# The queries' rank as a seven-product unit, and the values of heads 2 and 3 computed early and parked in memory

## The chip, the cores and the metric

The kernel runs on one core of a Trainium2 chip. Its engines work in parallel, each through its own list in order, and wait for each other by semaphores: TensorE (PE) does matrix products into PSUM, VectorE (DVE) and ScalarE (ACT) do everything elementwise, GpSimd (POOL) does a little, and SyncE (SP) issues the transfers between memory and the on-chip buffer, also in order. The metric is device time in microseconds (us) of one execution.

## The reference

One layer of a hybrid encoder over 512 tokens of width 2048. The input is normalised to `h`, and one wide projection makes all that follows:

```python
proj = h @ w_in[layer]
(a_q, a_f, a_i, a_g, c_q, c_kv, k_idx_raw, w_idx_raw, b_g, m_a, m_b) = jnp.split(proj, SPLIT_POINTS, axis=-1)
y_a = hgrn2_branch(a_q, a_f, a_i, a_g, ...)          # 8 heads of 128
y_b = dsa_branch(c_q, c_kv, k_idx_raw, w_idx_raw, b_g, ...)
merged = sigmoid(m_a) * (y_a @ w_pa) + sigmoid(m_b) * (y_b @ w_pb)
out = rmsnorm(x + merged @ w_out)
```

Branch A is a gated linear recurrence: per head a state is decayed by `f` and fed with `k` and the values `v` (`a_i`), in chunks. Branch B is sparse attention. The queries' rank `c_q` (512 wide) is normalised by its root mean square and projected to the attention's queries and the indexer's; the latent `c_kv` (256 wide) is normalised and projected to keys and values; the indexer's key `k_idx_raw` (128 wide) goes through a layer norm. The indexer scores all keys for each query, and the best 128 are kept.

## The kernel before

Everything is held transposed: features on the partitions, tokens along the free dimension. Products in float32 are done as three products of halves: each operand is split into a high part (`hi`, a rounded copy made by ACT) and a low part (`lo`, the difference, made by DVE); `mm3` (L93) adds high by high, high by low and low by high. `split` (L89) is that pair of instructions.

**Jobs and pumps.** The program is a list of jobs that are run one after the other. A job is a projection: it loads weights in blocks through SP (`load`, two raw buffers), splits them two blocks ahead of their use (`prep`, three buffers for each half), and issues the products block by block. After each part of a block it calls `pump` (L221), which issues pending loads and stores and moves each of the *lanes* one step on. A lane is a queue of generators with the work that runs beside the projections: norms, the recurrence of two heads (`hgrn_gen`, L767), the selection of the best keys (`top_gen`), attention (`att_gen`). So the order on each engine is written by hand, in steps of a pump. The recurrence has 17 steps. `top_gen` gets 2.7 credits a pump less `R.load`, which the recurrence sets to what its step costs on DVE, and spends 0.94, 1.21 or 1.48 on each of 48 selection steps.

**Kinds of job.** `feat_job` makes tiles of 128 features by 512 tokens, 48 products of 512 columns each; `ai_job` makes the values of two heads with tokens on the partitions, 192 products of 256 columns. `pair_job` (`pair_unit`, L1192) makes four feature tiles at once with seven products where eight would be needed: features and tokens are cut in two and sums of the quarters are multiplied, in all 336 products of 256 columns. It needs sums of the weights (`pair_sums`, L158) and sums of x (`pair_gen`, L1144: eight pieces, `s0` to `s7`, in three steps each). Its results are combined by seven DVE instructions, and stored (`pair_evac`, L1217).

**The order around the change.** A start stage written out by hand normalises x and makes the values of heads 0 and 1. Then come `feat_job`s for half of the rank, the indexer's key, the other half of the rank, and the latent, with the sums of x, the norm of the key and the sum of squares of the rank beside them; the seven-product units of the gates and of heads 4 to 7 (13 units; the normalised rank is reloaded and split beside the third and fourth); the indexer; `end_index`; values of heads 6 and 7, values of 4 and 5, `f` and `q` of heads 0 and 1, values of 2 and 3, `f` and `q` of heads 2 and 3; `open_att` (L1300), which drains all recurrences but one and puts the attention's buffers where theirs lay; the attention's queries (`uq_evac`) and keys and values (`ukv_job`) of two heads; one job of gates (`gate_job`, L1246) with a hook that drains the last recurrence; the output projections.

Four PSUM banks (`mmp`) turn over among the tiles of all jobs; four more (`sdp`) serve the lanes.

Of the kernel before, what the change touches and what calls it, by code (L numbers as in the profile page):

```python
# [63 lines left out]
EVEN = 0  # L64
MO = (0, 128, 384, 768)
# [3 lines left out]
def hybrid_block(ctx, tc, x, norm_w, w_in, lb_table, gnorm_a, q_norm_w, kv_norm_w, w_uq,  # L69
# [51 lines left out]
    cq_d = dram.tile([4, 128, T], F32, name="cq_d")  # L121
    qf_d = dram.tile([2, 4, 128, T], F32, name="qf_d")
# [400 lines left out]
    def cq_evac(j0):  # L523
        def evac(c, ps):
            t = R.cq[:, j0 + c, :]
            A.activation(t, ps, AF.Copy)
            late[1].append(lambda: SP.dma_start(cq_d[j0 + c], t))
        return evac

    def kx_evac(c, ps):  # L530
        A.activation(R.kx[:, 0, :], ps, AF.Copy)

    def ckv_evac(c, ps):
        t = R.g.tile([128, 2, 256], F32, name=f"c{c}").rearrange("p a b -> p (a b)")
        A.activation(t, ps, AF.Copy)
        late[1].append(lambda: SP.dma_start(ckv_d[c], t))
# [7 lines left out]
    def q_sums(j0):  # L544

        for j in (j0, j0 + 1):
            s = R.i.tile([128, T], F32, name="nsq", bufs=2)
            A.activation(s, R.cq[:, j, :], AF.Square)
            if j == 0:
                R.qs = R.i.tile([128, T], F32, name="qs")  # L550
                first = s
            elif j == 1:
                V.tensor_add(R.qs, first, s)
            else:
                V.tensor_add(R.qs, R.qs, s)
        if j0 == 0:
            yield
            return
        sh = R.i.tile([128, T], FR, name="sumh")
        sl = R.i.tile([128, T], FR, name="suml")  # L560
        split(sh, sl, R.qs)
        yield
        yield
        ps = bank("ns")
        mm(ps, ones_r, sh, True, False)
        mm(ps, ones_r, sl, False, True)
        rstd_row(ps, 512, R.rq)
        yield
# [43 lines left out]
    def kidx_gen():  # L612
        def spread(src):
            sh = R.i.tile([128, T], FR, name="sumh")
            sl = R.i.tile([128, T], FR, name="suml")
            split(sh, sl, src)
            yield
            ps = bank("ns")
            mm(ps, ones_r, sh, True, False)
            mm(ps, ones_r, sl, False, True)  # L620
            return ps

        ps = yield from spread(R.kx[:, 0, :])
        t = R.i.tile([128, T], F32, name="nt", bufs=2)
# [1041 lines left out]
```

## Time and profile before

| | us |
|---|---|
| median of 3 runs | 1343.94 (1342.82 to 1344.22) |
| profiled execution | 1345.55 |
| its span, first to last instruction | 1343.8 |
| PE busy | 1331.4 (99%) |
| DVE busy | 1088.4 (81%) |
| ACT busy | 691.4 (51%) |
| transfers | 202.10 MB, mean 150 GB/s |

The profile is of one execution. A row of its timeline gives the start and the duration of one instruction in microseconds, the engine, the line of the kernel, the operation and what it writes and reads (`out<-in`, buffer numbers left out); in square brackets stands how long the engine had been idle before, and what it waited for. Neighbouring matmuls overlap in such rows, so that start to start is the price of one. A row of windows gives the stretch, its length, then for PE, PEld (weight loads), DVE, ACT and POOL the busy time with the number of instructions, the granted clock of PE as a share of full speed, the share of the transfer engines and GB/s.

### The profile page before, as it was taken

The page shows a single profiled execution, that of the slowest core. Times are in us where ns is not written, and L with a number is a line of the kernel's source. Part 1 is how long each engine was busy: PE and PEld are TensorE (multiplying, and loading weights), DVE is VectorE, ACT ScalarE, POOL GpSimd, SP SyncE. Part 2 cuts the span into 40 slices and gives each one's busy share as a digit, 9 for nine tenths or more (in the row PEclk, how much of TensorE's full clock was granted, in tenths as well). Part 3 has the DMA queues.
Part 4 walks back from the last instruction along what each step waited for, and adds up shares of the span by engine and source line. Part 5 has one row for each costly group of instructions (what it writes and reads, how often), then busy time and mean ns, then how long its engine had stood idle before and what let it go on. Part 6 is the DMA issues. An engine that isn't in the chain of part 4 may idle for free.

```text
span 1343.8 us, 27088 instructions
## 1 busy us (share of the span) xinstructions
PE 1331.4 (99%) x11058; PEld 1243.0 (93%) x11058; DVE 1088.4 (81%) x1764; ACT 691.4 (51%) x1115; POOL 51.7 (4%) x63
## 2 busy tenths in 40 slices
PE   8999999999999999999999999999999999999997
PEld 8888999999999999999999898888888888899996
DVE  7978889988898888886778887975656658899997
ACT  7555445545554445445756554655433434354455
POOL 0000000000000000000000000020101100001112
PEclk9999999999999999999999999999999999999999
DMA  7245345544453454446214433445856556654643
GB/s 226 71 118 145 108 142 173 158 141 142 127 154 105 138 154 142 143 143 207 85 51 140 132 106 96 126 136 172 289 167 202 181 187 212 212 174 148 194 145 126
DMA packets 143326, 202.10 MB, mean 150 GB/s; under 512 B 10545, under 2 KB 83810, under 8 KB 143074
## 3 DMA queue, kind: packets, MB, share of 16 engines
q1 hardware_dynamic: 142914, 200.12, 47.5%
q8 instruction: 86, 1.41, 0.4%
q14 instruction: 38, 0.31, 0.1%
q10 hardware_dynamic: 288, 0.26, 0.1%
HBM read 166.25 MB, written 35.66 MB: 150 GB/s over the span
## 4 chain that ended last, share of the span: by engine, by line
PE 97%; DVE 1%; DMA 0%; ACT 0%; issue 0%; SPq 0%; DVEq 0%; ACTq 0%
PE pp L94 16%; PE pp L95 16%; PE pp L96 16%; PE acc L94 14%; PE acc L96 13%; PE acc L95 13%; PE acc L99 2%; PE hl L99 1%; PE ho L99 1%; PE sc L94 1%; PE sc L95 1%; PE sc L96 1%; DMA x<-in_x_dram 0%; PE pt L374 0%; PE hp L99 0%; PE po L96 0%
## 5 line engine op out<-in xcount | busy, mean ns | idle before, releaser
L171 ACT ACTIVATE wh<-sv 128x512 fp32r<-128x512 f32 x264 | 158.6, 625 | 114.4 <-DVE sv L164 85.4
L169 ACT ACTIVATE bh<-wr 128x768 fp32r<-128x768 f32 x132 | 111.5, 845 | 197.6 <-issue 91.8
L95 PE MATMUL pp<-s,wh 128*128 128x256 f32 x624 | 172.6, 277 | 0.0
L94 PE MATMUL pp<-s,wh 128*128 128x256 f32 x624 | 172.6, 277 | 0.0
L96 PE MATMUL pp<-s,wl 128*128 128x256 f32 x624 | 172.6, 277 | 0.0
L173 DVE TENSOR_TENSOR wl<-sv,wh 128x1024 fp32r<-128x1024 f32 x132 | 161.2, 1221 | 5.4
L172 DVE TENSOR_TENSOR bl<-wr,bh 128x768 fp32r<-128x768 f32 x132 | 126.0, 954 | 37.7 <-ACT bh L169 37.3
L94 PE MATMUL acc<-xh,wh 128*128 128x512 f32 x304 | 121.0, 398 | 0.0
L96 PE MATMUL acc<-xh,wl 128*128 128x512 f32 x304 | 118.8, 391 | 0.0
L95 PE MATMUL acc<-xl,wh 128*128 128x512 f32 x304 | 118.6, 390 | 0.0
L95 PEld LDWEIGHTS pp<-s,wh 128*128 128x128 f32 x624 | 117.2, 188 | 0.0
L96 PEld LDWEIGHTS pp<-s,wl 128*128 128x128 f32 x624 | 117.2, 188 | 0.0
L94 PEld LDWEIGHTS pp<-s,wh 128*128 128x128 f32 x624 | 117.2, 188 | 0.0
L95 PE MATMUL pp<-xl,bh 128*128 128x256 f32 x416 | 115.1, 277 | 0.0
L96 PE MATMUL pp<-xh,bl 128*128 128x256 f32 x416 | 115.0, 277 | 0.0
L94 PE MATMUL pp<-xh,bh 128*128 128x256 f32 x416 | 115.0, 277 | 0.0
L91 DVE TENSOR_TENSOR wl<-wr,wh 128x1024 fp32r<-128x1024 f32 (+1 forms) x70 | 84.0, 1201 | 28.8 <-ACT wh L90 28.7
L90 ACT ACTIVATE wh<-wr 128x1024 fp32r<-128x1024 f32 (+1 forms) x70 | 72.3, 1033 | 61.6 <-PE acc L95 38.1
L164 DVE TENSOR_TENSOR sv<-wr 128x512 f32<-128x512 f32 x132 | 92.7, 702 | 10.3 <-DMA wr<-in_w_in_dram 6.9
L94 PE MATMUL acc<-yh,wh 128*128 128x512 f32 x256 | 100.3, 392 | 0.0
L96 PE MATMUL acc<-yh,wl 128*128 128x512 f32 x256 | 99.9, 390 | 0.0
L95 PE MATMUL acc<-yl,wh 128*128 128x512 f32 x256 | 99.9, 390 | 0.0
(391 smaller groups left out, 3769.9 us busy)
## 6 DMA issues: line engine op xcount, KB each, us to landing
wr<-in_w_in_dram SPq DMA_DIRECT2D x136, 512.0 KB, 3.7
wr<-in_w_out_dram SPq DMA_DIRECT2D x28, 512.0 KB, 3.9
mg<-gate_d SPq DMA_DIRECT2D x48, 256.0 KB, 5.3
gate_d<-c SPq DMA_DIRECT2D x44, 256.0 KB, 5.2
wr<-in_w_in_dram SPq DMA_DIRECT2D x36, 256.0 KB, 3.1
wr<-in_w_pa_dram SPq DMA_DIRECT2D x16, 512.0 KB, 5.4
wr<-in_w_pb_dram SPq DMA_DIRECT2D x16, 512.0 KB, 4.0
wr<-in_w_qidx_dram SPq DMA_DIRECT2D x8, 512.0 KB, 4.5
```

Source lines behind the costliest of these rows:

```text
L90: A.activation(hi, src, AF.Copy)
L91: V.tensor_tensor(lo, src, hi.bitcast(F32), op=OP.subtract)
L94: PE.matmul(ps, lh, rh, start=first, stop=False, skip_group_check=True)
L95: PE.matmul(ps, lh, rl, start=False, stop=False, skip_group_check=True)
L96: PE.matmul(ps, ll, rh, start=False, stop=last, skip_group_check=True)
L99: PE.matmul(ps, l, r, start=first, stop=last, skip_group_check=True)
L164: V.tensor_tensor(sv[:, 0:2, :], b[:, 1:3, :], b[:, 0:1, :].to_broadcast([128, 2, 256]), op=OP.add)
L169: A.activation(bh, b[:, 1:4, :], AF.Copy)
L171: A.activation(vh[:, i:i + 2, :], sv[:, i:i + 2, :], AF.Copy)
L172: V.tensor_tensor(bl, b[:, 1:4, :], bh.bitcast(F32), op=OP.subtract)
L173: V.tensor_tensor(vl, sv, vh.bitcast(F32), op=OP.subtract)
```

## The change

- The rank's four feature tiles are no longer two `feat_job`s but one `pair_job`, the first seven-product unit. Its raw result goes to memory (`cq_d`) as before.
- The jobs behind the start are now the latent, the indexer's key, the values of heads 2 and 3 (`ai_job(1, early=True)`, with its weights split as in the other jobs), then the unit of the rank.
- The early values are stored in memory (`v_d`) and loaded when the recurrence of heads 2 and 3 begins. Their job behind the indexer is gone.
- The sums of x are made in two steps a piece, seven pieces before the first unit (`pair_early`) and the eighth inside it (`pair_late`).
- The indexer's key is stored (`kx_d`); its norm, the sum of squares of the rank (`q_squares`, from reloaded pieces) and the scaling of the rank (`q_rows`, unchanged) run one after the other beside the units of the gates, in buffers that are free there.
- The selection starts one job earlier, ahead of the values of heads 6 and 7, with 2.9 credits a pump, less one while the latent's norm runs.
- The attention's first queries are computed ahead of `open_att` and held in PSUM; `open_att` evacuates them, and fixes the order of the attention's buffers.

```diff
+    def q_squares():
+        for j0 in (0, 2):
+            for _ in range(3):
+                yield
+            ts = [R.g.tile([128, 2, 256], F32, name=f"c{i}").rearrange("p a b -> p (a b)") for i in range(2)]
+            for i, t in enumerate(ts):
+                SP.dma_start(t, cq_d[j0 + i])
+            yield
+            yield
+            for t in ts:
+                A.activation(t, t, AF.Square)
...
+        sh, sl = R.cqh[:, 3, :], R.cql[:, 3, :]
+        split(sh, sl, R.rq)
+        yield
+        ps = row_sums(sh, sl)
...
-                    credit += 2.7 - R.load
+                    credit += 2.9 - R.load - bool(lanes["norm"])
...
+            if early:
+                for i in range(2):
+                    t = R.g.tile([128, 2, 256], F32, name=f"c{i}")
+                    A.activation(t, ps[i].rearrange("p (t n) -> p t n", t=2), AF.Copy)
+                    SP.dma_start(v_d[:, 2 * i:2 * i + 2, :], t)
+                return
...
+        if p == 1:
+            hg[p, "v"] = R.v.tile([128, 4, 256], F32, name="hv", bufs=2)
+            SP.dma_start(hg[p, "v"], v_d)
...
+    def pair_early():
+        for k in range(EARLY):
+            a = R.i.tile([128, 2, T], F32, name="xa", bufs=2)
+            V.tensor_tensor(a, *pair_rows(k), op=OP.add)
             d = R.i.tile([128, 4, 256], F32, name="sv", bufs=2)
+            pair_sums_of([a[:, i, j:j + 256] for i in (0, 1) for j in (0, 256)], [d[:, i, :] for i in range(4)])
+            yield
+            hi, hi4, lo, lo4 = sums_place(k)
             df = d.rearrange("p q n -> p (q n)")
+            split(hi, lo, df[:, 0:768] if hi4 is not None else df)
...
+            yield
+
+    def pair_late():
+        for k in range(EARLY, 8):
+            ae, ao, da, db = (R.g.tile([128, 2, 256], F32, name=f"c{i}") for i in range(4))
...
     lane("misc", lb_gen)
-    lane("misc", pair_gen)
-    feat_job(w_in, 4096, 2, NK, 4, x_rhs, cq_evac(0))
-    lane("norm", lambda: q_sums(0))
+    lane("misc", pair_early)
+    feat_job(w_in, 4608, 2, NK, 4, x_rhs, ckv_evac)
     feat_job(w_in, 4864, 1, NK, 4, x_rhs, kx_evac)
-    lane("norm", kidx_gen)
-    feat_job(w_in, 4352, 2, NK, 4, x_rhs, cq_evac(2))
-    lane("norm", lambda: q_sums(2))
-    feat_job(w_in, 4608, 2, NK, 4, x_rhs, ckv_evac)
+    ai_job(1, early=True)
+    lane("misc", pair_late)
+    pair_job(w_in, [4096, 4352], NK // 2, x_pair, pair_evac([cq_d[0:2], cq_d[2:4]], [None, None]))
+    for gen in (kidx_gen, q_squares, q_rows):
+        lane("norm", gen)
...
         leave("norms")
         R.a = enter("att")
+        for n in ("aq0", "av0", "av1", "ak0", "aq1", "ak1"):
+            R.a.tile([128, 2, T] if n[1] != "v" else [128, 4, 256], FR, name=n)
+        for c, ps in enumerate(held):
+            uq_evac(0)(c, ps)
...
     jobs.append(end_index)
+    lane("top", top_gen)
     ai_job(3)
-    lane("top", top_gen)
     ai_job(2)
     af_aq(0)
-    ai_job(1)
     af_aq(1)
+    held = []
+    uq_job(0, lambda c, ps: held.append(ps))
     jobs.append(open_att)
-    uqkv(0)
+    ukv_job(0)
```

More of the change, by code (lines that the diff above doesn't have):

```diff
@@ L520, in lb_gen @@
         yield
[L523 to L528, printed above, removed]
     def kx_evac(c, ps):
[L531 removed]
+        t = R.i.tile([128, T], F32, name="kx")
+        A.activation(t, ps, AF.Copy)
+        late[1].append(lambda: SP.dma_start(kx_d, t))
     def ckv_evac(c, ps):
[L534 removed]
+        t = R.i.tile([128, T], F32, name=f"ck{c}")
         A.activation(t, ps, AF.Copy)
@@ L542, in rstd_row, with row_sums @@
         return r
[L544 to L553, printed above, removed]
-            else:
-                V.tensor_add(R.qs, R.qs, s)
-        if j0 == 0:
-            yield
[L558 to L563, printed above, removed]
+    def q_squares():
[9 more added lines that the diff above has]
+                A.activation(t, t, AF.Square)
+            if j0 == 0:
+                V.tensor_add(R.rq, *ts)
+            else:
+                V.tensor_add(ts[0], *ts)
+                V.tensor_add(R.rq, R.rq, ts[0])
+            for _ in range(3):
+                yield
[3 more added lines that the diff above has]
+        ps = row_sums(sh, sl)
+        for _ in range(2):
+            yield
+        rstd_row(ps, 512, R.rq)
+        for _ in range(5):
+            yield
+    def row_sums(sh, sl):
         ps = bank("ns")
@@ L612, in kidx_gen @@
     def kidx_gen():
[L613 to L616, printed above, removed]
+        t, parts = R.rq, (R.cqh[:, 2, :], R.cql[:, 2, :])
+        SP.dma_start(t, kx_d)
+        for _ in range(3):
             yield
[L618 to L624, printed above, removed]
-        V.scalar_tensor_tensor(t, ps, -1.0 / 128, R.kx[:, 0, :], op0=OP.mult, op1=OP.add)
-        s = R.i.tile([128, T], F32, name="nsq", bufs=2)
+        split(*parts, t)
+        yield
+        ps = row_sums(*parts)
+        for _ in range(2):
+            yield
+        V.scalar_tensor_tensor(t, ps, -1.0 / 128, t, op0=OP.mult, op1=OP.add)
+        for _ in range(4):
+            yield
+        s = R.g.tile([128, 2, 256], F32, name="c3").rearrange("p a b -> p (a b)")
         A.activation(s, t, AF.Square)
+        split(*parts, s)
         yield
-        ps = yield from spread(s)
-        r = rstd_row(ps, 128)
+        ps = row_sums(*parts)
+        for _ in range(2):
+            yield
+        rstd_row(ps, 128, s)
         yield
-        V.scalar_tensor_tensor(t, t, c_iw, r, op0=OP.mult, op1=OP.mult)
+        V.scalar_tensor_tensor(t, t, c_iw, s, op0=OP.mult, op1=OP.mult)
         V.tensor_scalar(t, t, c_ib, None, op0=OP.add)
         split(R.kih, R.kil, t)
+        yield
         yield
@@ new lines, in pair_early @@
+            df = d.rearrange("p q n -> p (q n)")
+            split(hi, lo, df[:, 0:768] if hi4 is not None else df)
+            if hi4 is not None:
+                split(hi4, lo4, df[:, 768:])
+            yield
+    def pair_late():
+        for k in range(EARLY, 8):
+            ae, ao, da, db = (R.g.tile([128, 2, 256], F32, name=f"c{i}") for i in range(4))
+            for i, a in enumerate((ae, ao)):
+                V.tensor_tensor(a.rearrange("p a b -> p (a b)"), *(x[:, i, :] for x in pair_rows(k)), op=OP.add)
+            pair_sums_of([a[:, j, :] for a in (ae, ao) for j in (0, 1)], [t[:, j, :] for t in (da, db) for j in (0, 1)])
@@ L1170, in pair_gen @@
             yield
+            hi, _, lo, _ = sums_place(k)
+            for i, d in enumerate((da, db)):
+                n = slice(i * 512, i * 512 + 512)
+                split(hi[:, n], lo[:, n], d.rearrange("p a b -> p (a b)"))
     def x_pair(k):
```

65 lines of the change are left out of this document (30 added, 35 removed).

## The prediction

> **What bounds the kernel now.** I read the engine totals first, then the chain that ended last.
>
> ```profile
> PE 1331.4 (99%) x11058; PEld 1243.0 (93%) x11058; DVE 1088.4 (81%) x1764; ACT 691.4 (51%) x1115; POOL 51.7 (4%) x63
> ...
> PE 97%; DVE 1%; DMA 0%; ACT 0%; issue 0%; SPq 0%; DVEq 0%; ACTq 0%
> ```
>
> TensorE (PE) streams from end to end: 97% of the chain. A matmul removed is its issue time gained; any place where PE has to wait for something new is lost in full. VectorE (DVE), at 81%, is the only engine that can make PE wait for long. So the question is what the change takes from PE, and where it leaves less cover over DVE's work.
>
> **The gain.** The timeline of PE gives the price of a 512-wide matmul: in the seventh job behind the indexer, 84 of them lie between these two starts. ScalarE (ACT) reads the first product of every seven-product unit as soon as the unit is through, so two such reads give a unit's length.
>
> ```profile
> 845.66 0.39 PE L94 MATMUL acc<-xh,wh 128*128 128x512 f32 x1
> ...
> 864.72 0.39 PE L94 MATMUL acc<-cqh,wh 128*128 128x512 f32 x1
> ```
> ```profile
> 193.29 0.58 ACT L1222 ACTIVATE c<-pp 128x512 f32<-128x512 f32 x1
> ...
> 231.41 0.58 ACT L1222 ACTIVATE c<-pp 128x512 f32<-128x512 f32 x1
> ```
>
> (864.72 - 845.66) / 84 = 0.2269 us for one; a unit takes 38.12 us, or 0.1135 us for each of its 336 matmuls of 256 columns. The rank had 4 tiles x 16 x 3 = 192 wide matmuls, 43.56 us; as a unit it costs 38.12. **Gain 5.44 us.** The value job that moves (192 matmuls of 256) costs PE 21.8 us in either place, and the six row-sum matmuls stay six. The rest is waits.
>
> **Wait 1, the head.** Before, eight sets of sums of x were made over 28 pumps in three steps each; now seven sets over the 16 pumps of the latent (two tiles), the key tile and half of the value job, in two steps. PE's cover per pump is 12 x 0.2269 = 2.72 us. These rows of DVE's timeline price its steps, and PE's row is where the stage begins.
>
> ```profile
> 50.21 1.23 DVE L91 TENSOR_TENSOR wl<-wr,wh 128x1024 fp32r<-128x1024 f32 x1
> ...
> 52.81 1.22 DVE L1148 TENSOR_TENSOR sv<-xh,xl 128x1024 f32<-128x1024 f32 x1
> ...
> 54.41 1.22 DVE L91 TENSOR_TENSOR wl<-wr,wh 128x1024 fp32r<-128x1024 f32 x1
> 55.54 0.42 DVE L1153 TENSOR_TENSOR sv<-sv 128x256 f32<-128x256 f32 x1
> ...
> 59.02 1.22 DVE L1148 TENSOR_TENSOR sv<-xh,xl 128x1024 f32<-128x1024 f32 x1
> ...
> 61.74 0.68 DVE L91 TENSOR_TENSOR wl<-wr,wh 128x512 fp32r<-128x512 f32 x1
> ...
> 68.15 0.42 DVE L1155 TENSOR_TENSOR sv<-sv 128x256 f32<-128x256 f32 x1
> ...
> 69.71 1.23 DVE L91 TENSOR_TENSOR s<-sv,s 128x1024 fp32r<-128x1024 f32 x1 [0.53 <-ACT s L90]
> ```
> ```profile
> 42.43 0.47 PE L94 MATMUL acc<-xh,wh 128*128 128x512 f32 x1
> ```
>
> A weight block of 1024 takes 1.13 us (54.41 to 55.54), one of 512 takes 0.68 - 0.08 = 0.60; the five adds and subtractions of a set 2.72 (59.02 to 61.74); its low part can't start before ACT has made the high part, 1.14 us behind the last subtraction (68.57 to 69.71), and takes 1.14. Set, weight block, low part in turn are so 2.72 + 1.22 + 1.14 = 5.08 us in two pumps of 5.45 us. DVE comes out of the start late, at 52.81, and now can hardly catch up. In program order: set 0 to 55.53, block 3, low 0 to 57.9; set 1 to 60.6, block 4, low 1 to 62.95; set 2 to 65.7, block 5, low 2 to 68.0; set 3 to 70.74, block 6 done at 71.4. PE, from 42.43, has the latent done at 64.2 (96 x 0.2269) and wants block 6, the key tile's third, at 69.66, its low half two matmuls later at 70.1: **1.3 us of waiting**. Low 3, block 7, set 4, then block 8 at 77.6; PE, now 1.3 late, wants it at 76.5: **1.1 us**. From there blocks cover 5.45 us each and DVE gains. Take 2.4; from 0 (if ACT's answer cost nothing, 0.6 us less in each turn) to 3.5.
>
> **The seven-product units.** The eighth set, the key norm and the squares of the rank add some 10 us to DVE and three row-sum chains, spread over five units.
>
> ```profile
> 120.40:311.00 190.60, 190.60 (x1680) 190.59 (x1679) 170.03 (x243) 94.93 (x151) 0.00 (x0) 1.00 0.49 147
> ...
> 800.00:860.00 60.00, 60.00 (x755) 51.85 (x755) 50.19 (x95) 33.91 (x52) 0.31 (x1) 1.00 0.35 107
> ```
>
> DVE has 20.6 us free in these 190.6 (five units), so 10 us fit; ACT is half idle, which covers its extra table loads; the parked rank and values use SP, where loads run two blocks ahead. The first `pair_late` write waits on DVE for the values' store out of the same tiles, with `pair_sums` of block 15 queued behind it; block 13 and 14 are split by then. Take 0.3, from 0 to 1.5. In the recurrence the selection gets two tenths more credit a pump; bounds 0 to 1.5, take 0.2, since it falls on idle time of DVE (9.8 us of 60 in the second row).
>
> **Wait 2, the opening of attention.** This is the step that decides. Behind the indexer there are now seven jobs, or 50 pumps, ahead of `open_att`: values 3, values 2, `af`/`aq` of 0 and 1 (six of eight pumps) and the queries' product (two). A recurrence takes 17 pumps, so three take 51: heads 0 and 1 do their last row sums in pump 49, scaling in pump 50, and the final split in `open_att` itself. Before, six pumps (16 us of PE) lay between that split and the queries' evacuation. PE reaches pump 49 at the same distance from the start of the recurrence as before, so the old clock serves:
>
> ```profile
> 844.73 0.40 PE L99 MATMUL hz<-hzh,ones_r 128*128 128x512 f32 x1
> ```
> ```profile
> 847.31 1.27 ACT L939 ACTIVATE hk<-hz,cols 128x512 f32<-128x512 f32 x2
> 848.59 1.28 ACT L940 ACT_TABLE_LOAD   x1
> 849.89 1.06 ACT L940 ACTIVATE hk<-hk 128x1024 f32<-128x1024 f32 x1
> ```
> ```profile
> 839.51 0.69 DVE L91 TENSOR_TENSOR hzl<-hk,hzh 128x512 fp32r<-128x512 f32 x1 [3.76 <-PE ho L99]
> ...
> 846.72 0.69 DVE L686 MAX8 m<-M 128x8 f32<-128x512 f32 x1
> ...
> 848.23 0.69 DVE L686 MAX8 m<-M 128x8 f32<-128x512 f32 x1
> ...
> 850.98 0.75 DVE L945 SCALAR_TENSOR_TENSOR hk<-ho,cols,hk 128x512 f32<-128x512 f32 x1
> ...
> 853.76 1.48 DVE L91 TENSOR_TENSOR hy<-hk,hy 128x512 fp32r<-128x512 f32 x2
> ...
> 868.69 0.69 DVE L966 SCALAR_TENSOR_TENSOR aq<-acc,aq 128x512 fp32r<-128x512 f32 x1
> ```
> ```profile
> 873.13 0.60 ACT L90 ACTIVATE ak<-acc 128x512 fp32r<-128x512 f32 x1 [0.61 <-PE acc L96]
> ```
> ```profile
> ya_d<-hy SPq DMA_DIRECT2D x16, 256.0 KB, 4.6
> ```
>
> PE's row sums end at 845.66, the queries' second tile 12 x 0.2269 later at 848.4, the two key tiles at 851.1; the value tile after that needs the PSUM bank in which the queries are held. DVE, in order from 839.51: low part 0.6; five selection steps of 1.51 (846.72 to 848.23), which by the credits end in pump 49, 7.55; two gatings of `aq`, now here, 1.2; two weight blocks 2.26; second low part 0.6: 851.7. Then scaling 2.78 (850.98 to 853.76), the split 1.4, the queries' low part 0.69: bank free at 856.6. **5.5 us of waiting.** Then the two value tiles, 2.7 us, to 859.3, and the gate job wants the bank of the first key tile. Its evacuation writes `ak0`, which by the order of the names lies where `hq` lay, from which the first low half of y is being stored: split 855.2, landing 4.6 later, ACT 0.60 and DVE 0.68: 861.1. **1.8 us more, 7.3 together.** Lowest: DVE free of the selection, ACT's chain alone (847.31 to 850.95, from 845.66) gives 849.3, the bank 854.2, 3.1 us, and the store covered; highest 9.
>
> **Wait 3, the end of the last recurrence.** The two pumps of the queries' product belonged to heads 2 and 3; their recurrence now starts two pumps (5.4 us) later against the gate job, whose hook drains it. Rows of three engines:
>
> ```profile
> 924.08 0.40 PE L99 MATMUL hz<-hzh,ones_r 128*128 128x512 f32 x1
> ```
> ```profile
> 927.33 1.06 ACT L940 ACTIVATE hk<-hk 128x1024 f32<-128x1024 f32 x1
> ...
> 933.74 1.29 DVE L91 TENSOR_TENSOR hy<-hk,hy 128x512 fp32r<-128x512 f32 x2
> ```
> ```profile
> 939.72 0.60 ACT L1249 ACTIVATE gs<-acc 128x512 f32<-128x512 f32 x1 [3.57 <-DMA ya_d<-hy]
> ```
> ```profile
> 942.04 0.41 DVE L91 TENSOR_TENSOR P<-tC,PT 128x256 fp32r<-128x256 f32 x1
> ```
> ```profile
> 942.52 0.39 PE L94 MATMUL po<-PT,av 128*128 128x512 f32 x1
> ```
>
> Before, from the row sums (924.08) to the second low half of y (935.03) it is 11 us; its store holds ACT at the gate's second tile until 939.72, the probabilities' split queues behind, and the product with the values (942.52) finds them 0.07 us old. After, row sums are at 929.5, ACT's chain ends 4.3 later (924.08 to 928.39), then 2.78 and 1.4 of DVE: 938.0, 3.0 us later than now, and all that stands behind comes **3.0 us later, with PE**. From 0 (if wait 2 has let DVE and ACT run ahead) to 4.5.
>
> **Sum.** -5.4 + 2.4 + 0.3 + 0.2 + 7.3 + 3.0 = +7.8 us. The profiled execution took 1345.55 us, its span 1343.8; that is 1.6 us above the median of the runs, 1343.94. So 1353.3 for an execution like the profiled one, **1351.7 us** for the median.
>
> **A rule on the clock.** The trace shows what an idle PE does to its clock:
>
> ```profile
> 1335.00:1340.00 5.00, 1.19 (x10) 0.98 (x9) 2.30 (x6) 2.58 (x8) 0.00 (x0) 0.82 0.63 235
> 1340.00:1344.00 4.00, 0.00 (x0) 0.00 (x0) 0.00 (x0) 0.00 (x0) 0.00 (x0) 0.50 0.59 223
> ```
>
> PE ended its work at 1336.2, and a mean of 0.82 over the 5 us means half speed for 1.8 of them: the clock fell 2 us after the last matmul. A wait of 5.5 us would let it fall too. How soon it rises again no row shows. If half speed lasts between nothing and the 5.5 us of the wait, it costs 0 to 2.75 us; taken by itself as a rival, 2 us. The Trainium skill (TensorE: Matmul & The Clock Gate, Part 1: The HAM clock gate) says that the clock is halved after an idle window of about 3.4 us and comes back after one busy window of as much: an estimate by that page is 1.7 us lost for each such gap. The fall in the trace agrees in kind, and came earlier than a whole window behind the last matmul.
>
> **The rivals.**
> 1. *The clock falls in wait 2.* For it: the two rows above. Against it: the wait may come in two pieces of 3 to 4 us with 2.7 us of work between them. +7.8 + 2 = +9.8: 1353.7.
> 2. *The head and wait 3 hide, wait 2 stands at its lowest.* For it: ACT is free for two fifths of its time or more in both rows of windows, so its answers may come sooner than walked. -5.4 + 0.5 + 3.1 to 4.9: -1.8 to 0, about 1343.
> 3. *Faster: the last recurrence is done when `open_att` comes.* One mechanism: if heads 0 and 1 are three pumps further on (17 steps each by the code, 51 against 50 pumps, is my count), split and store fall behind 8.2 us of PE's work, both 3.1 and 1.8 us vanish, and heads 2 and 3 start in the queries' pumps as before, which takes wait 3 away. It decides from two pumps on. Then -5.4 + 2.4 + 0.5 = -2.5, with the head hidden -5: 1339 to 1341.4. Against it: 17 pumps lie between the row sums of one recurrence and the next also in this trace.
> 4. *The selection ends late.* It needs 16 x (0.94 + 1.21 + 1.48) = 58.1 credits; 50 pumps at 2.9, less 27.4 of load per recurrence and 8 for the latent's norm, give just that in pump 49. One step over, and attention starts a pump later, is drained ahead of the second queries' job, and PE waits through a softmax of 4 to 6 us more: +13, 1357.
> 5. *The change doesn't do what it says*: the rank as a unit costs more than any other. Its instructions are those of the gates; no chance of weight.
>
> **How the numbers follow.** Forecast 0.58 (own range 1347 to 1357), clock 0.13, late selection 0.06, near even 0.13, faster 0.10. A difference of 0.2%, 2.7 us, is what a measurement of this kernel can tell from none. Slower 0.76 (forecast, clock, late selection, less a small part of the forecast's low end), same 0.14, faster 0.10. Lowest sum of all bounds -2.3, which is 1341.6; highest +14.6. Range 1341.5 to 1357, which leaves out most of the faster case and the far end of the late ones.
>
> **What would show it.** Right: units of 38.1 us, the first ending some 73 us after the key tile begins; PE idle 1 to 1.5 us before its third key block and about 1 us at the start of the early values, ended by DVE's `wl`; one wait of 4 to 6 us at the first value product of the first `ukv` job, ended by the queries' low part (L966 before), and one of 1 to 2 at the gate job's first tile, ended by `ak`, with ACT idle ahead of `ak` on the store of y; about 3 us in all at transposes or `po` near the end of the gate job. Wrong: PE without idle rows between the queries' product and the gate job, or the sums' rows no denser in the head. Below 1341 the last recurrence was not late; above 1357 the selection or the clock was.

## The result, and the profile after

The changed kernel takes 1351.79 us (median of 4 runs, 1351.11 to 1353.56) against 1343.59 us before (median of 4 runs, 1342.82 to 1344.22): a ratio of 1.0063, 95% interval 1.0046 to 1.0081. It is slower by 8.2 us; the forecast was 7.8. That the total came out so near is partly luck: three terms of the sum were wrong, in both directions.

The engine totals and the shares of the chain of waits, on the page after:

```profile
PE 1327.1 (98%) x11202; PEld 1244.6 (92%) x11202; DVE 1110.1 (82%) x1805; ACT 698.7 (52%) x1129; POOL 54.1 (4%) x63
...
PE 91%; DVE 5%; ACT 2%; DMA 1%; issue 1%; SPq 0%; DVEq 0%; ACTq 0%
```

PE is busy for 4.3 us less than before and the span is 6.0 us longer (1349.8 against 1343.8). The chain, which lay on PE for 97%, now crosses DVE for 5% and ACT for 2%. What PE waited for, from the view of waits after (engine, line, what it waited for: us in total, times, longest):

```profile
PE acc L95 <- DVE aq L984: 5.4, 1, 5.4
PE pp L95 <- DVE c L1262: 1.9, 2, 1.1
...
PE acc L97 <- DVE wl L92: 1.2, 1, 1.2
PE acc L96 <- DVE wl L92: 0.9, 1, 0.9
...
PE pp L95 <- ACT c L1257: 0.7, 1, 0.7
PE acc L95 <- ACT gs L1285: 0.6, 1, 0.6
```

The stages, as windows (length, then busy time of PE, PEld, DVE, ACT and POOL with counts, then the granted clock, the DMA share and GB/s). Before: the head (from the first job behind the start to the first unit), the seven-product units, the first queries, keys and values, the gate job.

```profile
42.43:120.40 77.97, 77.97 (x345) 64.24 (x343) 63.72 (x101) 43.47 (x60) 0.00 (x0) 1.00 0.37 103
120.40:616.12 495.72, 495.72 (x4369) 495.71 (x4368) 429.55 (x612) 242.07 (x381) 0.00 (x0) 1.00 0.47 141
...
864.72:877.24 12.52, 12.52 (x190) 10.76 (x189) 10.83 (x16) 6.28 (x9) 0.00 (x0) 1.00 0.48 141
877.24:939.76 62.52, 62.01 (x620) 52.31 (x619) 39.74 (x87) 36.65 (x67) 6.98 (x8) 1.00 0.47 156
```

The same four after:

```profile
41.48:99.02 57.54, 55.38 (x339) 48.82 (x338) 53.02 (x87) 26.38 (x38) 0.00 (x0) 1.00 0.40 115
99.02:637.85 538.83, 536.26 (x4713) 535.46 (x4711) 466.83 (x670) 274.14 (x425) 0.00 (x0) 1.00 0.46 141
...
862.90:882.52 19.62, 14.21 (x65) 12.20 (x64) 18.01 (x30) 11.30 (x15) 0.00 (x0) 0.83 0.42 133
882.52:946.52 64.00, 63.38 (x749) 53.22 (x747) 43.53 (x90) 36.67 (x67) 9.29 (x8) 1.00 0.48 162
```

The third row of each is the opening of attention. Before, PE was busy for the whole of the first three. After, it idles for 2.2 us in the head, 2.6 in the units and 5.4 at the opening of attention, where the granted clock is 0.83 as well. If each gap between two starts is measured against the usual step (0.2269 us for 512 columns, 0.1135 for 256), which also counts short gaps and slow matmuls, it is 2.7, 3.6 and 7.5 us more than before. These three are the loss; the gate job's one wait is 0.78 us, against 0.68 of another one before.

**The head.** PE's timeline, and DVE's:

```profile
69.03 0.39 PE L96 MATMUL acc<-xl,wh 128*128 128x512 f32 x1
70.63 0.50 PE L97 MATMUL acc<-xh,wl 128*128 128x512 f32 x1 [1.21 <-DVE wl L92]
...
77.24 0.39 PE L96 MATMUL acc<-wl,xh 128*128 128x256 f32 x1 [0.88 <-DVE wl L92]
```
```profile
69.89 0.68 DVE L92 TENSOR_TENSOR wl<-wr,wh 128x512 fp32r<-128x512 f32 x1
```

The step from 69.03 to 70.63 is 1.38 us too long: the low half of the key tile's third block is made from 69.89 to 70.57. At the first early-values block 1.15 us are lost, and 0.23 just before it.

**The opening of attention.** PE, DVE and ACT, then two windows:

```profile
871.85 0.39 PE L97 MATMUL acc<-ckh,wl 128*128 128x512 f32 x1
877.65 0.58 PE L95 MATMUL acc<-wh,ckh 128*128 128x256 f32 x1 [5.41 <-DVE aq L984]
878.03 0.41 PE L96 MATMUL acc<-wl,ckh 128*128 128x256 f32 x1
878.24 0.41 PE L97 MATMUL acc<-wh,ckl 128*128 128x256 f32 x1
```
```profile
871.70 0.68 DVE L696 MATCH_REPLACE8 M<-m,M 128x512 f32<-128x512 f32 x1
...
872.75 0.74 DVE L963 SCALAR_TENSOR_TENSOR hk<-ho,cols,hk 128x512 f32<-128x512 f32 x1
...
876.91 1.28 DVE L984 SCALAR_TENSOR_TENSOR aq<-acc,aq 128x512 fp32r<-128x512 f32 x2
```
```profile
868.91 1.06 ACT L958 ACTIVATE hk<-hk 128x1024 f32<-128x1024 f32 x1
...
878.62 1.09 ACT L91 ACTIVATE ak<-acc 128x512 fp32r<-128x512 f32 x2 [0.43 <-DMA ya_d<-hy]
```
```profile
871.80:877.60 5.80, 0.44 (x2) 0.02 (x1) 5.61 (x10) 2.59 (x5) 0.00 (x0) 0.79 0.33 123
877.60:881.90 4.30, 4.25 (x20) 4.25 (x21) 3.67 (x5) 2.27 (x4) 0.00 (x0) 0.50 0.66 199
```

ACT has the factors of the last recurrence ready at 869.97 us, DVE is busy with the last two steps of the selection until 872.75, then it scales, splits, and makes the queries' low part; PE waits for that. And the 20 products that follow start every 0.213 us instead of 0.1135: the clock is at half. A mean of 0.79 over 5.80 us is half speed for the last 2.4 of them, so the clock fell about 3.0 us after the last matmul, and it came back 4.3 us after the first new one. The Trainium skill (TensorE: Matmul & The Clock Gate, Part 1: The HAM clock gate) has about 3.4 us for each of the two, counted in windows that run on by themselves; the half speed of this trace, 2.4 and 4.3 us, is as long as two such windows, but the clock fell sooner than a whole window behind the last matmul. The last section has more executions.

**The end of the gate job** (ACT's timeline after; before, ACT stood 3.57 us at the second gate tile for the store of y):

```profile
945.87 1.14 ACT L1285 ACTIVATE gs<-acc 128x512 f32<-128x512 f32 x2
```

No wait on a store is left there, and PE lost 0.78 us.

### The profile page after: what moved, and what is told of

The parts are those of the page before. It is cut to its first block, busy times and chain, and to the rows that moved or that the text cites. A ratio compares the mean times of both kernels' runs of the same rounds, so it can differ in the third digit from the quotient of the medians.

```text
span 1349.8 us, 27460 instructions
## 1 busy us (share of the span) xinstructions
PE 1327.1 (98%) x11202; PEld 1244.6 (92%) x11202; DVE 1110.1 (82%) x1805; ACT 698.7 (52%) x1129; POOL 54.1 (4%) x63
## 4 chain that ended last, share of the span: by engine, by line
PE 91%; DVE 5%; ACT 2%; DMA 1%; issue 1%; SPq 0%; DVEq 0%; ACTq 0%
PE pp L95 16%; PE pp L97 16%; PE pp L96 16%; PE acc L95 11%; PE acc L97 11%; PE acc L96 11%; PE hl L100 1%; PE ho L100 1%; PE acc L100 1%; DVE xl L390 1%; PE sc L95 1%; PE sc L96 1%; PE sc L97 1%; DMA fr<-in_w_in_dram 0%; DVE wl L92 0%
## 5 line engine op out<-in xcount | busy, mean ns | idle before, releaser
L174 ACT ACTIVATE wh<-sv 128x512 fp32r<-128x512 f32 x280 | 169.2, 626 | 132.8 <-DVE sv L167 90.4
L95 PE MATMUL pp<-s,wh 128*128 128x256 f32 x672 | 185.8, 276 | 1.9 <-DVE c L1262 1.9
L96 PE MATMUL pp<-s,wh 128*128 128x256 f32 x672 | 185.5, 276 | 0.0
L97 PE MATMUL pp<-s,wl 128*128 128x256 f32 x672 | 185.5, 276 | 0.0
L176 DVE TENSOR_TENSOR wl<-sv,wh 128x1024 fp32r<-128x1024 f32 x140 | 171.0, 1221 | 4.9
L95 PEld LDWEIGHTS pp<-s,wh 128*128 128x128 f32 x672 | 126.1, 188 | 2.2 <-issue 2.2
L97 PEld LDWEIGHTS pp<-s,wl 128*128 128x128 f32 x672 | 126.2, 188 | 0.0
L96 PEld LDWEIGHTS pp<-s,wh 128*128 128x128 f32 x672 | 126.2, 188 | 0.0
L95 PE MATMUL pp<-xh,bh 128*128 128x256 f32 x448 | 123.8, 276 | 0.7 <-ACT c L1257 0.7
L95 PE MATMUL acc<-xh,wh 128*128 128x512 f32 x240 | 96.2, 401 | 0.0
L97 PE MATMUL acc<-xh,wl 128*128 128x512 f32 x240 | 93.9, 391 | 1.2 <-DVE wl L92 1.2
L96 PE MATMUL acc<-xl,wh 128*128 128x512 f32 x240 | 93.5, 390 | 0.0
```

What stands on the lines that cost most here:

```text
L95: PE.matmul(ps, lh, rh, start=first, stop=False, skip_group_check=True)
L96: PE.matmul(ps, lh, rl, start=False, stop=False, skip_group_check=True)
L97: PE.matmul(ps, ll, rh, start=False, stop=last, skip_group_check=True)
L174: A.activation(vh[:, i:i + 2, :], sv[:, i:i + 2, :], AF.Copy)
L176: V.tensor_tensor(vl, sv, vh.bitcast(F32), op=OP.subtract)
```

## The experiments

All are edits of the changed kernel (1351.79 us).

**1. Two empty pumps in the early sums.** In `pair_early`:

```diff
             yield
+            if k == 1:
+                yield
+                yield
```

> The changed kernel with two empty pumps put behind the second set of the early sums (the last of the seven sets is done at the 16th pump instead of the 14th). Forecast's theory: PE waited 1.4 us at the key tile's third weight block and 1.4 us in two pieces at the first block of the early values because DVE makes the low part of a block only behind the sets of sums queued ahead of it; with one set less ahead of those blocks both waits are gone, the stage from the latent's first product to the first product of the first seven-product unit shrinks from 57.5 us to 54.8, and the time falls by 2.7 us, from 1351.8 to 1349.1. Rival: the weights themselves come late (the DMA or ACT's high part): then both waits stay, and the time stays within 1 us of 1351.8. Rival: the early values become the place that waits, since the sets end nearer to them: then some 2 us of waiting turn up in the value job's later blocks.

Measured: 1351.22 us (1350.54 to 1351.7). The trace has no wait left in the head, and the stage took 55.37 us instead of 57.54. So the order of DVE's queue was the cause. But the time fell by 0.6 instead of 2.7: in the profiled execution 1.0 us came back ahead of the queries' product (0.7 of it in one stop of PE at 719 us for nothing that the profile shows) and 0.4 at the opening of attention, where the half clock lasted for 5.5 us of work instead of 4.3. Executions of one kernel lie that far apart (the changed one's by 2.4), so the median is no proof of the 2.2 us; the trace of the head is.

**2. The key's last step cut in two.** In `kidx_gen`:

```diff
         V.scalar_tensor_tensor(t, t, c_iw, s, op0=OP.mult, op1=OP.mult)
+        yield
         V.tensor_scalar(t, t, c_ib, None, op0=OP.add)
         split(R.kih, R.kil, t)
         yield
-        yield
```

> The changed kernel with the indexer key's last step cut in two: bias and split (1.2 us of DVE, and 0.7 us in which DVE waits for ACT's high part) move one pump later, behind the evacuation of the unit. Theory: PE waited 0.9 us at the last block of the third unit and 1.3 us at its first products of the next one because the key's last step stood in DVE's queue just ahead of the unit's last weights and its evacuation; about 1.9 us less stand there now, so these two waits, 2.1 us together, shrink to 0.3 or less: 1349.8 against 1351.8. The wait of 0.9 us near 411 us, with the last step of the rank's norm, stays. Rival: the seven steps of the evacuation (0.6 to 0.7 us each) hold the banks in any unit in which DVE has had no idle time, whatever the step: then the wait only moves to the next unit, and the time stays within 0.7 us of 1351.8.

Measured: 1351.58 us (1351.18 to 1351.75), no gain. PE's timeline of this run near the eighth unit's end:

```profile
407.21 0.39 PE L95 MATMUL pp<-xh,bh 128*128 128x256 f32 x1 [1.02 <-ACT c L1257]
...
411.48 0.36 PE L95 MATMUL pp<-s,wh 128*128 128x256 f32 x1 [1.11 <-DVE c L1262]
```

The waits at 214 and 218 us shrank from 2.1 to 0.3 us, as the theory had it; but 1.2 us appeared at 406 and the one at 410 grew from 0.9 to 1.3. The rival was right on the time, though the wait moved five units on and not to the next. What held the later place was still open; experiment 9 bears on it.

**3. Three more pumps ahead of attention.** In `ai_job`, called with `extra=3` for heads 4 and 5:

```diff
-                    if k % 2 == 1:
+                    if k % 2 == 1 or k == 2 and i < extra:
                         pump()
```

> The changed kernel with three more pumps in the value job of heads 4 and 5 (one more in each of three blocks), so that 53 pumps instead of 50 lie ahead of the opening of attention. Forecast's theory: the last recurrence is late by the count of pumps (51 steps against 50); now its row sums come about two to three pumps (5 to 8 us) sooner, the queries are evacuated before PE wants their bank, the wait of 5.6 us before the first value product of attention is gone, and with it the half clock behind it (2.0 us): 7.6 us less, 1344.2 against 1351.8; the last recurrence of heads 2 and 3 starts as far ahead of the gate job as before the change, and the wait of 0.8 us at the end of the gate job goes too. Rival: the selection's steps on DVE hold the scaling of the recurrence, whatever its pumps: then a wait of 2 to 3 us is left, 1347 to 1349. Rival: heads 2 and 3's products and the selection only come together more densely, and DVE, with no idle time in these stages, gives the gain back: 1350 or more.

Measured: 1363.21 us (1361.36 to 1364.69), 11.4 slower: the theory's remedy failed, and by far more than the last rival's least (1350). ACT's and PE's timelines:

```profile
883.58 1.09 ACT L91 ACTIVATE ak<-acc 128x512 fp32r<-128x512 f32 x2 [6.71 <-DMA ya_d<-hy]
```
```profile
886.69 1.06 PE L100 MATMUL hl<-hqs,hk 128*32 128x16 f32 x64 [4.98 <-DVE hqs L823]
```

The wait for the queries' bank did shrink, from 5.6 to 1.4 us. What came next in line took its place: the store of y that lies under the first key tile held ACT for 6.7 us, DVE's low part of the keys stood behind ACT, the first decay of the last recurrence behind that, and PE waited 5.0 us for it. Shorter waits, of 1.0 to 2.5 us at four other places from the recurrence of heads 0 and 1 to the end of the gate job, and half clock behind two waits come on top.

**4. Work for PE inside the wait.** In `ukv_job`, ahead of the value products:

```diff
+            if p == 0:
+                pw = bank("pw")
+                for i in range(22):
+                    mm(pw, ones_r, R.ckh[:, 0, :], i == 0, i == 21)
```

> The changed kernel with 22 matmuls of 512 columns on data already in place (their result is read by nobody) between the key products and the value products of attention's first key and value job: 22 x 0.2269 = 5.0 us of work for PE inside its wait of 5.6 us. Theory (the clock as a cost of its own): the value products ran at a granted clock of 0.50, one every 0.213 us instead of 0.1135, only because PE had been idle; with PE busy the clock stays at 1.00, PE waits only 0.6 us for the queries' bank, which comes free at the same time, and the 20 slow products save 20 x 0.1 = 2.0 us: 1349.8 against 1351.8. Rival: behind the value products PE has to wait for the bank of the first key tile anyway, which hangs on the store of y: then the saving comes back as a wait ahead of the gate job's first tile, and the time stays within 0.5 us. Rival: the half clock has another cause: then the rows stay at 0.213 us and the time is 1351.8 or a little more.

Measured: 1350.34 us (1349.31 to 1353.08). PE's timeline, and the window of the value products:

```profile
877.54 0.39 PE L95 MATMUL acc<-wh,ckh 128*128 128x256 f32 x1 [0.44 <-DVE aq L984]
```
```profile
877.50:880.50 3.00, 2.96 (x24) 2.96 (x25) 2.97 (x5) 2.27 (x4) 0.00 (x0) 1.00 0.58 208
```

The bank comes free at the same time, the clock stays at 1.00, and the stretch from the first queries' product to the gate job is 1.9 us shorter (17.74 against 19.62). No wait for the key tile's bank took the saving back. The half clock was a cost of its own, and idleness caused it. The times of the four executions overlap with those of the changed kernel, but their mean clocks do not: 0.998 to 0.999 against 0.996 in all four of the changed kernel.

**5. The selection ends sooner.** In `top_gen`:

```diff
-                    credit += 2.9 - R.load - bool(lanes["norm"])
+                    credit += 3.2 - R.load - bool(lanes["norm"])
```

> The changed kernel with a credit of 3.2 instead of 2.9 a pump for the selection, so that its 48th and last step falls, counted by the credits, in pump 44 instead of pump 49. Theory (two causes in wait 2): DVE took up the scaling of the last recurrence at 872.75 us, 2.8 us after ACT had its factors ready (869.97), because two steps of the selection stood ahead of it in DVE's queue; without them the wait of 5.6 us at the first value product of attention shrinks to some 2.8 us, and is then too short for the clock to fall, so that the 2.0 us of half clock go too: 1347.0 against 1351.8. Rival (the count of pumps alone): the chain from the row sums through ACT sets the time, the wait stays at 5 us or more, and the time within 1 us of 1351.8. Rival: the steps, put more densely, make DVE late within the recurrences, and a wait of 1 us or more turns up there.

Measured: 1352.26 us (1348.54 to 1352.6; the profiled execution is the fastest). PE's timeline of that one:

```profile
822.55 0.74 PE L100 MATMUL hl<-hqs,hk 128*32 128x16 f32 x64 [0.38 <-DVE hqs L823]
...
830.35 0.74 PE L100 MATMUL hl<-hq,hk 128*32 128x16 f32 x64 [0.75 <-DVE hk L836]
...
876.28 0.39 PE L95 MATMUL acc<-wh,ckh 128*128 128x256 f32 x1 [2.67 <-DVE aq L984]
```

Wait 2 is 2.83 us instead of 5.57 and the products behind it run at full clock: the selection's share was 2.74, as worked out. The last rival came in too: the recurrences of heads 0 and 1 lost 2.6 us. By the median nothing was gained: the three other executions were 3.4 to 4.1 us slower than the profiled one; their mean clock was 0.996 to 0.998 against 0.999, which would fit a half clock, but they left no trace that shows where.

**6. More pumps, other places.** The third experiment's edit, and in `open_att`:

```diff
-        for n in ("aq0", "av0", "av1", "ak0", "aq1", "ak1"):
-            R.a.tile([128, 2, T] if n[1] != "v" else [128, 4, 256], FR, name=n)
+        for n in ("aq0", "ay0", "ay1", "av0", "PT", "ak0", "ak1", "aq1", "av1"):
+            R.a.tile({"v": [128, 4, 256], "y": [128, T], "T": [128, 1280]}.get(n[1], [128, 2, T]), FR, name=n)
```

> The kernel with three more pumps (1363.2 us), and with the tiles of attention laid out so that queries, keys and values no longer lie where the low halves of y are being stored from; in those two places lie tiles that are wanted only later. Theory: there the wait behind the queries was replaced by the next one, ACT's first evacuation of a key tile, which waited 6.7 us for the store of y; behind it stood the values' evacuation on ACT and the first decay of the last recurrence on DVE (idle for 4.7 us), for which PE waited 5.0 us, with 1 us of half clock behind it. With the places apart these 6 us go: 1357, and lower by up to 4 us more if the waits of 2.4 us and the half clock at the end of the gate job are the same delay handed on. Rival: DVE's own queue (scaling, split, queries, decay) is late anyway: PE's wait for the decay stays at 3 us or more, and the time at 1360 or more.

Measured: 1357.41 us (1354.66 to 1359.21), as the theory had it. PE's timeline:

```profile
880.91 0.73 PE L100 MATMUL hl<-hqs,hk 128*32 128x16 f32 x64 [0.23 <-DVE hqs L823]
```

ACT starts the keys at 875.73 us without a wait, and the 5.0 us on PE are gone, so the store under the keys was their cause. Waits of 2.1 us (at the transposes of the last recurrence's keys) and 2.5 (end of the gate job) remain, as in experiment 3 (1.5 and 2.5). Before the second, DVE idles 7.35 us for ACT's softmax and then has the softmax's scaling ahead of the recurrence's; no experiment took these two waits apart.

**7. The rank as wide tiles again.** Ahead of the early values, in place of the unit:

```diff
...
+    for j0 in (0, 2):
+        feat_job(w_in, 4096 + 128 * j0, 2, NK, 4, x_rhs, cq_evac(j0))
     ai_job(1, early=True)
...
-    pair_job(w_in, [4096, 4352], NK // 2, x_pair, pair_evac([cq_d[0:2], cq_d[2:4]], [None, None]))
```

> The changed kernel with the queries' rank taken out of its unit again and made as four wide tiles (192 matmuls of 512 columns) between the indexer key's tile and the early values; the parking of rank, key and values, the later norms and the order of everything behind stay as in the changed kernel. Theory (the gain by itself): 192 x 0.2269 = 43.6 us of wide matmuls come in for a unit of 38.1, and the waits stay where they were: 5.4 us more, 1357.2 against 1351.8. Rival: the wide tiles give DVE a cover that the unit doesn't, so that waits of the head and of the first units (2.8 and 2.1 us) shrink: 1355 or less, down to 1352, and the gain of the unit is mostly paid back by them.

Measured: 1355.25 us (1354.86 to 1355.76), 3.5 more. From the first rows of the stages, the head is 44.0 us longer (101.52 against 57.54) and the units 40.0 shorter (498.84 against 538.82). Wide tiles of 43.6 us went in and a unit of 38.1 out, so the 5.4 us of the gain are there; 1.9 us less are waited for in the units and 0.4 more in the head. The unit is worth its 5.4 us of PE and pays a part of them back in waits.

**8. Three edits together:** experiment 1, a credit of 3.2, and the places of experiment 6.

> The changed kernel with the two empty pumps in the early sums, the credit of 3.2 and the other places for attention's tiles together. Theory: the head's 2.2 us, 2.8 us of wait 2 and the 2.0 us of half clock go, and no store stands under the keys: 1351.8 - 7.0 = 1344.8, level with the kernel before (1343.3); by the first run, where 1.6 of the head's 2.2 us came back as longer waits in the recurrence, 1346.4. Rival: DVE is the limit of the whole stretch from the first recurrence to the gate job, and what is saved in one place is waited for in the next: 1349 or more.

Measured: 1349.99 us (1348.66 to 1352.46), as the rival had it. The head is 55.37 us and wait 2 is 2.83, but 2.8 us are lost in the recurrences, as in experiment 5, and the clock fell in the wait, which made the opening of attention 1.3 us longer than in experiment 5 (16.27 against 14.98).

**9. The rank's rows two units later.** Experiment 2, and in `q_rows`:

```diff
     def q_rows():
+        for _ in range(16):
+            yield
```

> The kernel with the key's last step cut in two (1351.6 us), and with the scaling and splitting of the rank's rows begun 16 pumps (two units) later. Theory (a collision on ACT, not DVE's mean load): where these rows stand now, the evacuation of the queries of heads 6 and 7 has just cost ACT two table loads and four gatings (4.9 us in one go, 375.9 to 380.8), which held the next block's high part and left DVE idle for 2.8 us; DVE then ran without a gap for 20 us and came late to the next evacuation, at which PE waited 0.9 to 1.3 us and, in the run with the cut step, once more 1.2. Two units later each evacuation needs one table only: those waits of 2.4 us go, the stretch of the units shrinks from 538.7 us to 536.3, and the time from 1351.6 to 1349.2. Rival (DVE's load): any unit into which the rows are put is overfull, the waits turn up there again, and the stretch stays at 538 us or more.

ACT's timeline of the changed kernel shows what stood ahead of the rows' unit:

```profile
375.87 1.28 ACT L1268 ACT_TABLE_LOAD   x1
377.17 1.15 ACT L1268 ACTIVATE c<-c 128x512 f32<-128x512 f32 x2
378.33 1.28 ACT L1268 ACT_TABLE_LOAD   x1
379.62 1.15 ACT L1268 ACTIVATE c<-c 128x512 f32<-128x512 f32 x2
```

Measured: 1348.64 us (1348.17 to 1349.28). The window of the units:

```profile
98.70:634.19 535.49, 535.49 (x4712) 535.13 (x4711) 466.28 (x670) 274.77 (x425) 0.00 (x0) 1.00 0.46 142
```

PE is busy for all of it, 3.2 us shorter than in experiment 2 (538.65) with the same work on DVE. So the rival falls: the norms do fit into the units' idle time, if they do not follow a burst of ACT. The burst itself was not taken away in any run; it is named as the cause because the waits went when only the rows moved.

**10. What holds, together.** Experiments 1, 2 and 9, a credit of 3.0, and experiment 4 with 8 matmuls.

> The changed kernel with the two empty pumps in the early sums, the cut step of the key, the rank's rows two units later, a credit of 3.0 (last step of the selection in pump 48, one pump ahead of the last row sums, instead of pump 49) and 8 matmuls (1.8 us) ahead of attention's first value products. Theory: head 2.2 us less, units 2.5 less, wait 2 down to some 2.8 us with the clock at 1.00 throughout (4.6 less), with the lower credit hardly denser in the recurrences than the changed kernel: 1351.8 - 9.3 = 1342.5, level with the kernel before or 1 us under it. Rival (DVE is the limit from the first recurrence to the gate job): up to 2.7 us of wait 2 come back within the recurrences, as with a credit of 3.2: 1345.

Measured: 1344.37 us (11 runs, 1343.27 to 1345.81) against 1343.13 before (21 runs): ratio 1.0007, interval 0.9998 to 1.0015, no difference that can be told. By the medians 7.4 us are recovered. It lies between theory (1342.5) and rival (1345): with the credit of 3.0 the stretch of the recurrences is still 1.0 us longer than in the changed kernel. Of PE's waits:

```profile
PE acc L95 <- DVE aq L986: 0.9, 1, 0.9
```

Here 8 x 0.2269 = 1.8 us of wait 2 are filled with products that nobody needs, so it is still 2.8 us long. No kernel of this study beats the one before.

**11. The same without the 8 matmuls.**

> The same kernel as the run before it, without the 8 matmuls. Theory: a wait of 2.8 us lies at the edge at which the clock falls, so that some of the executions have 1 to 2 us of half clock behind it and others none; its median lies 0 to 2 us above the run with the matmuls, and its executions lie further apart. Rival (the clock doesn't fall in so short a wait): the two are alike within 0.5 us.

Measured: 1344.31 us (10 runs, 1342.42 to 1345.6): the medians are alike, and the spread is somewhat wider. In the profiled execution the clock fell:

```profile
871.20:874.00 2.80, 2.78 (x14) 2.78 (x15) 2.77 (x4) 1.83 (x4) 0.00 (x0) 0.59 0.56 207
```

PE had waited 2.7 us, as in the profiled executions of experiment 5, where the clock stayed up, and of experiment 8, where it fell; the stretch from the queries' product to the gate job is 1.5 us longer than with the matmuls. So in a wait of this length it may fall or not, and over many executions it doesn't show in the median.

**12. Traffic ahead of the last stores.** In `hgrn_gen`, ahead of the last step (`junk_d` is a buffer in memory that nobody reads):

```diff
+        for j in (0, 1) if p == 1 else ():
+            late[1].append(lambda j=j: SP.dma_start(junk_d[j], w_in[0:128, j * 1024:(j + 1) * 1024]))
```

> The changed kernel with two copies of 512 KB between places in memory put into SP's queue just ahead of the last four stores of y (heads 2 and 3); nobody reads the copies. Theory (wait 3 fell away because the stores landed early): before the change the load of a weight block of 512 KB was issued 0.5 us ahead of these stores, they took some 4 us or more to land, and ACT's second gate tile stood 3.6 us behind one of them; after it, the last load was 5.5 us old, the stores took 2 to 3.5 us, and ACT did not wait. With 1 MB ahead of them again the stores land 3 us or more later, ACT waits 2 to 4 us at the gate tiles, PE's wait of 0.8 us at the end of the gate job grows to 3 or 4, and the time goes from 1351.8 to 1354.3. Rival (the gate tiles of the changed kernel lie on no tile that is being stored): ACT and PE wait no longer than before, and the time stays within 0.7 us of 1351.8.

Measured: 1352.93 us (1351.45 to 1353.44), the gate job 64.00 us as without. The copies went out at 937.06 and the stores only from 942.12 on, 5 us later, so most of the traffic was probably past, and the question of the landing was hardly put. ACT's timeline still shows one thing:

```profile
946.65 0.60 ACT L1288 ACTIVATE gs<-acc 128x512 f32<-128x512 f32 x1 [0.37 <-DMA ya_d<-hy]
```

The second gate tile does lie on a tile that is being stored, so the rival's reason falls; the time lies between the two (1351.8 and 1354.3). The store is just landing when ACT comes. By the semaphore it is the one issued at 943.81, which so took some 2.7 us; before the change the one that ACT waited for took 4.3 (issued at 935.35). Why it lands sooner stays open.

## Why the prediction was right, and where it was not

**Gain, -5.44: right.** The page after has 144 matmuls more, 336 narrow for 192 wide. A unit takes 38.12 us:

```profile
519.98 0.58 ACT L1257 ACTIVATE c<-pp 128x512 f32<-128x512 f32 x1
```
```profile
558.10 0.58 ACT L1257 ACTIVATE c<-pp 128x512 f32<-128x512 f32 x1
```

Experiment 7 found the 5.4 us and, beside them, the cover that the wide tiles had given.

**Wait 1, +2.4: right,** in place and size: 1.38 and 1.38 us for 1.3 and 1.1. Experiment 1 took both away by what stood in DVE's queue.

**Units, +0.3 (0 to 1.5): wrong, 3.6.** The step that failed is "DVE has 20.6 us free in these 190.6 (five units), so 10 us fit; ACT is half idle, which covers its extra table loads". It reasoned with means. ACT and DVE of the changed kernel, ahead of the third unit's end:

```profile
203.09 1.28 ACT L538 ACT_TABLE_LOAD   x1
204.39 0.69 ACT L538 ACTIVATE c<-ns,cols 128x512 f32<-128x512 f32 x1
205.09 1.28 ACT L539 ACT_TABLE_LOAD   x1
...
206.93 0.83 ACT L172 ACTIVATE bh<-wr 128x768 fp32r<-128x768 f32 x1
```
```profile
207.79 0.96 DVE L175 TENSOR_TENSOR bl<-wr,bh 128x768 fp32r<-128x768 f32 x1 [1.86 <-ACT bh L172]
```

Two table loads and two functions keep ACT for 3.8 us in one piece; the next block's high part stands behind them, DVE idles 1.86 us for it, and then has the key's step and an evacuation to make. DVE's idle time cannot be saved up: it is time in which DVE waits for ACT. Experiment 2 moved the key's last step behind the evacuation and experiment 9 the rows away from such a burst; together 3.3 of the 3.6 us were gone. The Trainium skill (ScalarE: Activation LUTs, What ACT_TABLE_LOAD costs) gives about 2.66 us to a switch of tables, a drain included; here the function starts 1.30 us after the load does, so the measured price is half of that, and the runs point to the place of the loads, not to their size.

**Selection, +0.2: right** for the changed kernel, which has no new wait in the recurrences. Experiment 5 shows how little was free there: a credit of 3.2 costs 2.6 us.

**Wait 2, +7.3: right by two errors.** The first piece was 5.57 us for 5.5, through the steps as walked: 2.74 of it are the selection's (experiment 5). The second, 1.8 us for the key tile's bank over the store of y, did not come: ACT waited 0.43 us for the store, PE not at all. In its place came rival 1, "the clock falls in wait 2", priced at 2 us: 2.0 in the trace after, 1.9 in experiment 4. The mechanism of the second piece is real all the same: with more pumps ahead of attention, the store under the key tile held ACT and, through DVE, PE for 5.0 us, and with the tiles apart this was gone (experiments 3 and 6).

The count of pumps behind it, 51 against 50, was right as a description and wrong as a lever: three more pumps made the kernel 11.4 us slower. Rival 3, by which the last recurrence is done when `open_att` comes, falls with the wait of 5.57 us; that three pumps would bring its 1339 to 1341 falls with experiment 3, though there the wait itself shrank to 1.4 us.

**Wait 3, +3.0 (0 to 4.5): wrong in size, 0.8,** and the gate job holds hardly more waiting than before, where 0.7 us were lost to another wait. DVE's chain did end late:

```profile
942.86 1.47 DVE L92 TENSOR_TENSOR hy<-hk,hy 128x512 fp32r<-128x512 f32 x2
```

Its end, 944.33, lies 61.8 us behind the gate job's start (882.52); before it was 57.8 (935.03 less 877.24), so 4.0 us later, even more than walked. But "all that stands behind comes 3.0 us later, with PE" failed: before, ACT reached the second gate tile early and stood 3.57 us for the store; after, it comes when the store is landing. Part of the chain's delay went into a wait that was there already.

**Rivals 2, 4 and 5.** Wait 3 nearly hid, but the head did not (2.7 us), and wait 2 was not at its lowest; the selection ended in its pump, ahead of the scaling at 872.75; and the rank's unit costs what the others cost.

**The account.** In the two profiled executions: -5.4 for the gain, +2.7 head, +3.6 units, +7.5 opening of attention, +0.2 from the gate job to the first product with y; the recurrences, the output job and the tail have 1.7 less, the start 0.9 less: 6.0. No term of the sum has these last 2.6, and no run looked for their cause. The medians differ by 8.2, because the profiled execution before (1345.55) was 2.0 us above the median of its runs, and the one after (1351.62) was not. So the forecast of 7.8 was met by 8.2 through three things that cancel: the terms that were wrong come to 0.8 more together, 2.6 less came from stages that the sum leaves out, and 2.2 more from which executions were profiled.

## What to carry to other kernels

Idle time of an engine in a mean is not room for new work: ask which engine it waits for there, and put new steps away from that one's bursts (here table loads on ACT). A wait taken away uncovers the next in line, so before moving work, list what each engine does next, and the stores that still read the places it wants to write. Here, with 21.8 us of PE's work taken out ahead of attention, the wait at its opening cost 7.5 us, more than the 5.4 that the unit saves; no run moved that work alone, and with the other steps put right the kernel only came level.

## What the runs showed of the hardware

A wait of 5.6 us cost 7.5 in the changed kernel, as the clock halved about 3 us into it and stayed so for 4.3 us of work. Six profiled executions hold this same wait (the changed kernel and experiments 1, 2, 7, 9 and 12), and in all of them the clock fell, but not at the same point: 2.3 to 5.0 us behind the end of the last matmul, with 2.8 to 5.5 us of half speed left for the work behind it; the stretch from the queries' product to the gate job took 18.96 to 20.03 us. So the price of one wait differs by 1 us from execution to execution. After waits of 2.7 us the clock fell in two profiled executions (experiments 8 and 11) and not in a third (experiment 5). The wait of experiment 8, and the work behind the wait of experiment 12:

```profile
872.63:875.30 2.67, 0.00 (x1) 0.00 (x1) 2.58 (x5) 2.01 (x4) 0.00 (x0) 0.91 0.49 178
```
```profile
878.12:881.12 3.00, 3.00 (x14) 3.00 (x15) 2.97 (x4) 1.66 (x4) 0.00 (x0) 0.53 0.59 201
```

A mean of 0.91 is half speed for the last 0.5 us of a wait of 2.67, so the clock fell 2.2 us behind the last matmul; a mean of 0.53 is half speed for 2.8 of the 3.0 us.

Stores of y, 256 KB each, took 4.0 to 4.9 us to land before the change (median 4.6) and 2.3 to 3.9 after it (median 3.4), with nothing changed in them; the profiles have the landing of 7 of the 16 stores before and of 4 after, and experiment 12 did not settle why they differ.
